# Modulation weights of a two-block network: one transfer and one tile for four k tiles instead of one

## The chip, the core and the metric

The kernel runs on one core of a Trainium2 chip, alone. The metric is device time in microseconds (us) of one execution of the whole program; lower is better. The engines of the core are named as the profile names them: PE is TensorE's matrix multiplication and PEld its weight load, DVE is VectorE, ACT is ScalarE, POOL is GpSimd, and SP is the engine from whose queue (SPq) nearly all DMA transfers of this kernel are issued, in order.

## The reference, cut to what matters

The whole network is a DiT-like stack of two blocks of two layers each (512 latent and 256 context tokens, model width 1024). Only the first layer of the first block, a gated delta net, is touched by the change. Ahead of every sublayer the reference modulates the normed tokens with shift, scale and gate vectors, which come from two conditioning vectors through a large matrix:

```
inputs['ada_w'] = nrm((DEPTH, D, 6 * D), D ** -0.5)     # [2, 1024, 6144], fp32: 48 MB
inputs['c'] = nrm((BATCH, D), 1.0)                      # conditioning of the latent tokens
inputs['c_ctx'] = nrm((D,), 1.0)                        # conditioning of the context tokens
...
shift, scale, gate, ... = split(silu(c) @ ada_w[l] + ada_b[l], 6)      # in words; for c and for c_ctx
```

So two vectors of 1024 numbers are multiplied with all of a 48 MB matrix. The product itself is tiny; what counts is that all 48 MB pass through SBUF and through the matrix engine once as moving data. The gated delta net around it projects the tokens to q, k, v and z (a 5-tap convolution and silu on q, k, v), and then runs a chunked recurrence over six chunks of 128 tokens in both directions, with a triangular inverse for each chunk.

## The kernel before, in words

**The modulation products.** The 12 sections of 1024 columns are made in 24 blocks of 512 columns (`ada_block`). A block needs the 1024 rows of the matrix, that is 8 k tiles of 128 rows. For each k tile, `raw_weights` (line 314 issues the transfer) loads a tile `araw` [128, 512] of 256 KB, and one fp32 product with a stationary operand of only 32 columns (`s4`, of which two columns are the two vectors) is made. k tile `kt` goes to column tile `kt % 4` of the array, 32 output partitions each, so that four products can run side by side if they stand next to each other in PE's queue and have their data. An fp32 product is two MATMUL instructions in the trace. All eight add up in one PSUM bank (`a`, in the first blocks also `g` or `i` by name), ACT copies the bank to `arow` (line 330), and four small products with `sel` add the four column tiles up. Every matmul of the kernel has line 163 (`mm`) and every transpose line 167.

**The buffers.** The first four blocks (shift and scale of the first layer, which everything waits for) take their tiles from the pool `stage`, 16 tiles of 256 KB. The other 20 blocks take theirs from `aw`, a ring of `ada_bufs` = 3 tiles. A tile is free again when its product is done, so from then on a new transfer waits on SPq for PE.

**Where the 20 blocks run.** They are `later` work: `deltanet` calls `fill(...)` between the projections, scans and inverses of the four pairs of heads, a block at a time (`ada_steps`). The order of the instructions on each engine is made by a scheduler ahead of the run, which moves the pieces among each other by priority (`scan_hp`, `inv_hp`) and by its own idea of when data is there. On the chip each engine then takes its list in order, and SPq issues its transfers in order too: what stands behind a waiting transfer waits with it.

**The other names.** `dn_project` makes q, k, v of two heads: PE products (g <- hh, wh and the like; high and low parts, 512 latent and 256 context tokens), then ACT and DVE convolve and apply silu. `sums` puts squares in a tile `acc` (one buffer), `dn_gate` puts silu(z) in `acc` too and stores it to DRAM (`zs`), and the convolved v stands in a tile `vT` (one buffer) until PE has transposed it (`dn_token_major`). `wr` are weights as loaded (ring of 2), `wh` and `wl` their high and low parts (made by ACT, line 203, and DVE, line 204; rings of 4). At the end `dn_output` fetches six heads' outputs from DRAM (`on`, two buffers, line 892; `z`, one buffer, line 894), multiplies them on DVE (line 895) and transposes them on PE; the last two heads go straight through `dn_direct`.

Of the kernel before, what the change touches and what calls it, by code (L numbers as in the profile page):

```python
# [21 lines left out]
P = 128  # L22
# [18 lines left out]
class Kernel:  # L41
    # how many steps of independent work go into the gaps of a chain, ring sizes, scheduling priorities
# [6 lines left out]
    ada_bufs = 3  # L49
# [18 lines left out]
    # ---------------------------------------------------------------- helpers  # L68
# [27 lines left out]
    def banks(self, **turns):  # L96
        """a tag takes the banks of these tags in turn (2: halves of s2)"""
        self.turns, self.rest = {k: itertools.cycle(v) for k, v in turns.items()}, None

    def psum(self, **nb):  # L100
        """(re)partition the 8 PSUM banks among tags"""
        if self.pb is not None:
            self.pb.release()
        self.nb = nb
        self.pb = self.pool("ps", 1, PSUM) if nb else None

    def setup(self):
# [17 lines left out]
        self.le = tri("le", -1, 1, ALU.is_ge)   # [p, f] = p <= f  # L125
        self.ge = tri("ge", 1, -1, ALU.is_ge)   # p >= f
        self.gt = tri("gt", 1, -1, ALU.is_gt)   # p > f
        self.lt = tri("lt", -1, 1, ALU.is_gt)   # p < f
# [5 lines left out]
    def open_w(self, raw, hi, unit, side):  # L134
        """rings of weight tiles: raw, high and low parts"""
        return unit, self.pool("wraw", raw, side=side), self.pool("whi", hi, side=side), self.pool("wlo", hi, side=side)
# [8 lines left out]
    def rsqrt(self, out, in_, mul, add, exponent=None):  # L145
        """out = (in_ * mul + add) ** -0.5 on GpSimd, tiny operands"""
# [11 lines left out]
    def exp_ln_tables(self):  # L158
        """the activation tables that hold both exp and ln, from here on"""
# [9 lines left out]
    def rows_to_cols(self, rows, tag, pool=None):  # L169
        """rows: DRAM APs [r, 128] -> const tile [128, sum r], whose columns self.finish_cols() fills"""  # L170
# [18 lines left out]
    def split(self, hi, lo, src, hi_eng):  # L189
        """hi + lo = src exactly, each with at most 12 significant bits"""  # L190
# [3 lines left out]
    def weights(self, src, a, mul=None):  # L194
        """DRAM view [128, a, unit // a] (times mul) -> hi, lo tiles of that shape"""
# [11 lines left out]
    # weights stationary: feature-major result, 256 output features at a time  # L207
# [3 lines left out]
    def gemm_steps(self, w, c0, groups, evac, ncol=256):  # L211
        """groups: lists of segments; a segment is (hi(kt), lo(kt), n). evac(j, [psum per segment])"""
# [12 lines left out]
    def ws_tile(self, ps, wk, j, segs, kts=range(NK)):  # L225
        """128 output features of the segments"""
# [6 lines left out]
    def gemm_halves(self, parts, segs):  # L233
        """the same of several (weights, first column, evac), where the last tokens come late: all products of the
        first segment go ahead"""
# [11 lines left out]
    # tokens stationary: token-major result, 512 output features at a time  # L247
# [14 lines left out]
    def ts_pair_steps(self, wk, hh, hl, t, out):  # L262
        """token tiles t, t + 1, 256 output features each, in the halves of a bank"""
# [16 lines left out]
    # ---------------------------------------------------------------- modulation  # L280
    def ada_setup(self):
# [11 lines left out]
        # column v of s4: vector v; the four column tiles of the array take a k tile each  # L293
# [3 lines left out]
        # sel[r, v]: rows that add up to vector v: v of each column tile, and the bias in row 2; then without the bias  # L297
# [10 lines left out]
    def raw_weights(self, src, a):  # L308
        if self.ada_own:
            raw = self.t(self.aw, [P, self.unit], "araw", bufs=self.ada_own)  # L310
        else:
            raw = self.t(self.stage, [P, self.unit], "araw", bufs=16)
        raw = raw.rearrange("p (a b) -> p a b", a=a)
        self.nc.sync.dma_start(out=raw, in_=src)
        return raw

    def ada_block(self, l, n, row):
        """products with columns n * 512 .. of ada_w[l] into row [128, 512], to be summed by sel"""
# [3 lines left out]
        per = self.unit // 512  # L322
        for u in range(NK // per):
            r0 = u * per * P
            raw = self.raw_weights(w[r0:r0 + per * P, n * 512:(n + 1) * 512].rearrange("(a p) m -> p a m", p=P), per)
            for a in range(per):
                kt = per * u + a
                r = slice(32 * (kt % 4), 32 * (kt % 4) + 32)
                self.mm(ps[r, :], self.s4[:, kt, :], raw[:, a, :], start=(kt < 4), stop=(kt >= 4))
        nc.scalar.copy(row, ps)  # L330

    def ada_cols(self, l, sec):
        """section sec of layer l, feature-major: [128, 8, 2] (lat, ctx)"""
# [13 lines left out]
    def ada_bc_store(self, l, sec, dst):  # L347
        """section sec of layer l to DRAM rows dst [2, 1024] (lat, ctx), to be read back on all partitions"""
# [12 lines left out]
    def load_bc(self, pool, row, tag, n=D):  # L361
        """a DRAM row [n] on all partitions"""
# [4 lines left out]
    # ---------------------------------------------------------------- gated delta net (layer 0)  # L367
# [3 lines left out]
    def load_transposed(self, x_src, ctx_src, xp):  # L371
        """the rows of x and ctx, feature-major: 8 tiles [128, 768]"""
# [21 lines left out]
    def deltanet(self, xp, xT, scratch, zs, gts, later):  # L394
        """normed, gated head outputs before norm_g go to scratch; returns the transposed y"""
# [7 lines left out]
        # shift, scale and the first products, in halves of the features  # L403
# [37 lines left out]
        # decay and beta  # L441
# [52 lines left out]
        def conv_silu2(blk, dst, ps):  # L494
            """dst = 2 silu(conv(x))"""
# [16 lines left out]
        for grp in range(4):  # L512
# [7 lines left out]
            # independent work for the gaps of the chains  # L520
# [26 lines left out]
    def dn_gate(self, half, w, hh, hl, onep, zs):  # L547
        """2 silu(z) of two heads, token-major, to DRAM"""
# [11 lines left out]
    def dn_project(self, grp, w, segs, one, onep, conv_silu2, beta, eg, fill, first):  # L560
# [8 lines left out]
        def sums(src, tag):  # L569
            """sums of squares per token, of twice the value"""  # L570
# [3 lines left out]
            # as rows, two chunks per column tile of the array; then transposed  # L574
# [32 lines left out]
        def ev_v(j, ps):  # L607
            vT = onep([P, W2], "vT", 1)
# [30 lines left out]
    def dn_tmp(self, one, shape):  # L639
        """one of a ring of 4 KB scratch tiles"""  # L640
# [8 lines left out]
    def dn_prepare(self, p, one, g):  # L649
        """inverses of both directions' triangular systems, and the q k products times the decays: their upper  # L650
        triangle is for direction 0, the lower one for direction 1"""
# [4 lines left out]
        for j, h in enumerate(heads):  # L656
            # decays between tokens j, i: a sum over an empty range in one of the two directions
# [34 lines left out]
    def dn_invert(self, Wt, one):  # L692
        """Wt[:, u] (unit triangular but for its diagonal; u < 12 upper, u >= 12 lower) -> its inverse, in place"""
# [7 lines left out]
        # [(b, i), u, j] -> [(b, u), i, j]: one matrix per partition  # L701
# [17 lines left out]
        # [0]: blocks of the inverse, [1]: their transposes; direction 0 was inverted transposed  # L719
# [8 lines left out]
        # 32 -> 64: source block row, target block row, per direction and pair  # L728
# [23 lines left out]
        # transposed 64-blocks: direction 0 in rows 0:64, direction 1 in rows 64:128  # L752
# [8 lines left out]
        # 64 -> 128  # L761
# [106 lines left out]
    def dn_store(self, p, O, one, scratch):  # L868
        """half the normed head outputs to DRAM"""
# [17 lines left out]
    # ---------------------------------------------------------------- shared pieces  # L887
    def dn_output(self, k, scratch, zs, yh, yl, yp, zp):
        """y = norm(o) * silu(z), transposed and split into yh, yl (norm_g applied on the way)"""
        nc = self.nc  # L890
        on = self.t(yp, [P, TOK], "on", bufs=2)
# [14 lines left out]
    def scaled_split(self, hi, lo, ps, scale):  # L906
        """hi + lo = ps * scale"""
# [39 lines left out]
    def proj_steps(self, w, xh, xl, k0, k1, tiles, evac, ncol=512):  # L947
        """token-major projection of k tiles k0 .. k1 of the transposed, split activations by w, in steps;
        evac(t, c0, psum[:, :ncol])"""
# [13 lines left out]
    def ln_stats(self, x, pool):  # L963
        """1 / std and mean per token"""
# [10 lines left out]
    def layernorm(self, x, pool):  # L975
        """x <- (x - mean) * rstd, per token"""
# [1287 lines left out]
```

## Time and profile before

| | |
|---|---|
| Time, median of three runs | 3865.22 us (3863.72 to 3866.85) |
| Profiled execution, first to last instruction (span) | 3858.7 us |
| PE busy over the span | 3740.8 us, 97% |
| DVE, ACT, POOL busy | 2343.5, 1541.7, 440.1 us |
| First 740 us of the span, where all modulation products run: PE busy | 701.67 us |
| ... of it with modulation products (araw) | 134.25 us |
| Transfers of araw | 192 of 256 KB |

The span is that of one profiled execution; the runs' median is 6.5 us above it. Times in the rows below are us from the span's start. PE "busy" is the time in which at least one matmul is under way; the matmuls are pipelined and overlap, so that what one costs the engine is read from the distance between its start and the start of what follows.

### The profile page before, as it was taken

What the parts mean: (1) busy time and instruction counts of PE and PEld (TensorE: products, weight loads), DVE (VectorE), ACT (ScalarE), POOL (GpSimd) and SP (SyncE); (2) the same over time, 40 slices, a digit from 0 to 9 for tenths busy, and PEclk for the clock granted to TensorE, in tenths of its full rate; (3) what the DMA queues carried; (4) which work ended last, traced back from release to release, by engine and by line L of the source; (5) the groups of instructions that cost most, each with busy time, mean ns of one, the idle gap of its engine ahead of it and who ended that gap; (6) DMA issues with size and microseconds to landing.
All of it is one profiled execution on the core that took longest, in us unless ns stands there. A gap on an engine that the chain in (4) does not pass through costs nothing.

```text
span 3858.7 us, 57682 instructions
## 1 busy us (share of the span) xinstructions
PE 3740.8 (97%) x23195; PEld 3033.0 (79%) x23195; DVE 2343.5 (61%) x3919; ACT 1541.7 (40%) x2836; POOL 440.1 (11%) x642
## 2 busy tenths in 40 slices
PE   8999999999999999998999999999999999999999
PEld 5675766888888877777888877788887888888887
DVE  3757655653333676677555656656666777556665
ACT  3444443332211244454222456544334655444332
POOL 3112211040000020003000102100000222100000
PEclk9999999999999999999999998999999999999999
DMA  4234234512122211113333213212332223223232
GB/s 166 77 96 132 88 118 126 175 61 66 56 65 66 69 59 33 34 50 91 98 97 91 86 55 106 65 60 88 99 96 86 72 67 106 87 66 93 91 95 82
DMA packets 248974, 329.47 MB, mean 85 GB/s; under 512 B 14408, under 2 KB 194988, under 8 KB 248705
## 3 DMA queue, kind: packets, MB, share of 16 engines
q1 hardware_dynamic: 248000, 325.40, 27.2%
q8 instruction: 182, 2.98, 0.3%
q14 instruction: 88, 0.71, 0.1%
q0 software_dynamic: 704, 0.37, 0.0%
HBM read 318.09 MB, written 7.63 MB: 84 GB/s over the span
## 4 chain that ended last, share of the span: by engine, by line
PE 83%; DVE 6%; ACT 4%; POOL 3%; issue 2%; DMA 1%; SPq 0%; ACTq 0%; POOLq 0%; DVEq 0%
PE g L163 41%; PE a L163 16%; PE o L163 13%; PE s L163 7%; PE i L163 2%; PE s L167 1%; PE a L167 1%; PE p L163 1%; DVE wl L204 1%; DMA araw<-in_ada_w_dram 1%; ACT wh L203 1%; ACT xr L1480 1%; ACT xr L1477 0%; DVE bst L968 0%; PE g L167 0%
## 5 line engine op out<-in xcount | busy, mean ns | idle before, releaser
L204 DVE TENSOR_TENSOR wl<-wr,wh 128x1024 fp32r<-128x1024 f32 (+1 forms) x508 | 587.6, 1164 | 435.8 <-ACT wh L203 420.8
L203 ACT CAST wh<-wr 128x1024 fp32r<-128x1024 f32 (+1 forms) x508 | 493.5, 981 | 783.6 <-PE o L163 373.1
L163 PE MATMUL g<-wh,fh 128*128 128x512 f32 x396 | 156.4, 395 | 0.0
L163 PE MATMUL g<-wh,fl 128*128 128x512 f32 x396 | 156.1, 395 | 0.0
L163 PE MATMUL g<-wl,fh 128*128 128x512 f32 x396 | 155.1, 392 | 0.0
L163 PE MATMUL g<-h2l,wh 128*128 128x512 f32 x352 | 138.0, 392 | 2.4 <-DVE h2l L1014 2.4
L163 PE MATMUL g<-h2h,wh 128*128 128x512 f32 x352 | 137.5, 392 | 0.0
L163 PE MATMUL g<-h2h,wl 128*128 128x512 f32 x352 | 137.1, 390 | 0.0
L163 PE MATMUL a<-araw,s 128*32 128x512 f32 x352 | 125.7, 617 | 6.2 <-DMA araw<-in_ada_w_dram 5.9
L163 PE MATMUL g<-hh,wh 128*128 128x512 f32 (+1 forms) x376 | 115.7, 363 | 1.7 <-ACT hh L421 1.5
L152 POOL TENSOR_SCALAR brs<-bmv 128x1 f32<-128x1 f32 x20 | 9.7, 484 | 932.1 <-DVE bmv L970 922.9
L163 PE MATMUL g<-hh,wl 128*128 128x512 f32 (+1 forms) x376 | 112.6, 358 | 3.5 <-DVE wl L204 3.5
L163 PE MATMUL g<-hl,wh 128*128 128x512 f32 (+1 forms) x376 | 114.0, 358 | 0.8 <-POOL hl L422 0.6
L1049 DVE TENSOR_TENSOR x<-g,x 128x512 f32<-128x512 f32 x120 | 82.5, 688 | 30.5 <-PE g L163 30.3
L163 PE MATMUL s<-k,q 128*128 128x384 f32 (+1 forms) x256 | 98.7, 440 | 0.0
L1186 DVE TENSOR_REDUCE nm<-s 128x1 f32<-128x768 f32 x64 | 61.1, 955 | 52.3 <-PE s L163 52.3
L163 PEld LDWEIGHTS g<-hh,wh 128*128 128x128 f32 x376 | 63.5, 193 | 35.5 <-issue 20.5
L163 PEld LDWEIGHTS g<-hl,wh 128*128 128x128 f32 x376 | 63.4, 192 | 32.6 <-issue 23.7
L163 PEld LDWEIGHTS g<-hh,wl 128*128 128x128 f32 x376 | 62.7, 192 | 32.4 <-issue 21.3
L163 PEld LDWEIGHTS g<-wh,fh 128*128 128x128 f32 x396 | 74.4, 188 | 17.4 <-ACT fh L2096 0.6
L1291 ACT CAST fh<-sg 128x768 fp32r<-128x768 f32 (+1 forms) x44 | 32.0, 726 | 138.9 <-DVE sg L1290 138.9
L163 PEld LDWEIGHTS g<-wl,fh 128*128 128x128 f32 x396 | 74.4, 188 | 16.6
(994 smaller groups left out, 11513.5 us busy)
## 6 DMA issues: line engine op xcount, KB each, us to landing
wr<-in_ffn_w_up_dram SPq DMA_DIRECT2D x132, 512.0 KB, 3.7
araw<-in_ada_w_dram SPq DMA_DIRECT2D x192, 256.0 KB, 3.1
wr<-in_ffn_w_down_dram SPq DMA_DIRECT2D x88, 512.0 KB, 3.7
wr<-in_ffn_w_gate_dram SPq DMA_DIRECT2D x44, 512.0 KB, 3.8
wr<-in_dn_w_in_dram SPq DMA_DIRECT2D x66, 256.0 KB, 2.8
wr<-in_xa_w_kv_dram SPq DMA_DIRECT2D x32, 512.0 KB, 3.9
wr<-in_hgrn_w_in_dram SPq DMA_DIRECT2D x32, 512.0 KB, 4.2
wr<-in_da_w_in_dram SPq DMA_DIRECT2D x24, 512.0 KB, 3.5
```

Of the source, the lines that this page charges most:

```text
L152: nc.gpsimd.tensor_scalar(out=out, in0=in_, scalar1=mul, scalar2=add, op0=MUL, op1=ADD)
L163: self.nc.tensor.matmul(out, lhsT=lhsT, rhs=rhs, start=start, stop=stop)
L167: self.nc.tensor.transpose(out, in_, self.ident[0:k, 0:k])
L203: nc.scalar.copy(hi, raw)
L204: nc.vector.tensor_tensor(out=lo, in0=raw, in1=hi.bitcast(F32), op=SUB)
L1049: nc.vector.tensor_tensor(out=a, in0=ps, in1=a, op=ADD)
L1186: nc.vector.tensor_reduce(out=nm, in_=s[cc][:, :, 0:384], axis=AX.XY, op=MAX, negate=True)
L1291: nc.scalar.copy(hi[j], sg[j])
L1480: nc.scalar.activation(y, x, AF.Copy, scale=rs)
```

## The change

A transfer now brings four k tiles at once: `araw` is [128, 4, 512], 1 MB, and a block takes two of them (`u` = 0 and 1). The four products of a tile go to the four column tiles of the array. There are 48 transfers instead of 192. The bytes, the products and what they add up to are the same. `stage` keeps its size (4 tiles of 1 MB for 16 of 256 KB). The ring in `aw` goes from three tiles of 256 KB to one of 1 MB. To make room for it, `vT` shares the one buffer of `acc`, and `on` has one buffer instead of two.

```
-    ada_bufs = 3
+    ada_bufs = 1
...
-    def raw_weights(self, src, a):
+    def raw_weights(self, src):
         if self.ada_own:
-            raw = self.t(self.aw, [P, self.unit], "araw", bufs=self.ada_own)
+            raw = self.t(self.aw, [P, 4, 512], "araw", bufs=self.ada_own)
         else:
-            raw = self.t(self.stage, [P, self.unit], "araw", bufs=16)
-        raw = raw.rearrange("p (a b) -> p a b", a=a)
+            raw = self.t(self.stage, [P, 4, 512], "araw", bufs=4)
         self.nc.sync.dma_start(out=raw, in_=src)
         return raw
...
-        per = self.unit // 512
-        for u in range(NK // per):
-            r0 = u * per * P
-            raw = self.raw_weights(w[r0:r0 + per * P, n * 512:(n + 1) * 512].rearrange("(a p) m -> p a m", p=P), per)
-            for a in range(per):
-                kt = per * u + a
-                r = slice(32 * (kt % 4), 32 * (kt % 4) + 32)
-                self.mm(ps[r, :], self.s4[:, kt, :], raw[:, a, :], start=(kt < 4), stop=(kt >= 4))
+        for u in range(2):
+            raw = self.raw_weights(w[512 * u:512 * u + 512, n * 512:(n + 1) * 512].rearrange("(a p) m -> p a m", p=P))
+            for a in range(4):
+                self.mm(ps[32 * a:32 * a + 32, :], self.s4[:, 4 * u + a, :], raw[:, a, :], start=(u == 0), stop=(u == 1))
...
-            vT = onep([P, W2], "vT", 1)
+            vT = onep([P, W2], "acc")
...
-        on = self.t(yp, [P, TOK], "on", bufs=2)
+        on = self.t(yp, [P, TOK], "on", bufs=1)
```

The scheduler makes a new order from this for the first fifth of the program. PE's list of 20359 instructions has 3431 that stand otherwise at its front; the last 16928 are the same in both, and the order on the other engines is the same behind the delta net too.

PE, fifth block of modulation products (the first from the ring in `aw`), among the products of a projection (g <- hh, wh are token products), before: some of the block's eight products stand alone or in twos.

```order
L163 MATMUL g_1736<-hh_56_263,wh_1713 128x512
L163 MATMUL g_1737<-hh_56_263,wh_1713 128x256
L163 MATMUL g_1736<-hl_64_271,wh_1713 128x512
L163 MATMUL a_1680<-araw_1693,s_12_112 32x512
L163 MATMUL a_1680<-araw_1696,s_12_112 32x512
L163 MATMUL g_1737<-hl_64_271,wh_1713 128x256
L163 MATMUL g_1736<-hh_56_263,wl_1714 128x512
L163 MATMUL g_1737<-hh_56_263,wl_1714 128x256
L163 MATMUL g_1736<-hh_57_264,wh_1719 128x512
L163 MATMUL a_1680<-araw_1699,s_12_112 32x512
L163 MATMUL g_1737<-hh_57_264,wh_1719 128x256
L163 MATMUL g_1736<-hl_65_272,wh_1719 128x512
```

PE, the same block after the change: the first four products stand together (x4), then come 29 token products (15 of 128x512 and 14 of 128x256, of which the last are shown), then the second four.

```order
L163 MATMUL g_1676<-hl_67_274,wh_1665 128x512
L163 MATMUL g_1677<-hl_67_274,wh_1665 128x256
L163 MATMUL g_1676<-hh_59_266,wl_1666 128x512
L163 MATMUL a_1632<-araw_1639,s_12_112 32x512 x4
L163 MATMUL g_1677<-hh_59_266,wl_1666 128x256
L163 MATMUL g_1676<-hh_60_267,wh_1665 128x512
```

What moved: products of k tiles that stood between token products now stand in fours. In 29 of the 44 fours behind the first two blocks nothing stands between the four; in 15 the first product stands apart from the other three. The first two blocks stand as eight in a row each.

SP, transfers at the same place, before: the ring's transfers of 256 KB, singly and in threes, among the weights `wr`.

```order
L200 DMA wr_1730<-in_dn_w_in_dram 128x2x256
L314 DMA araw_1693<-in_ada_w_dram 128x512
L314 DMA araw_1696<-in_ada_w_dram 128x512
L314 DMA araw_1699<-in_ada_w_dram 128x512
L200 DMA wr_1907<-in_dn_w_in_dram 128x2x256
L314 DMA araw_1702<-in_ada_w_dram 128x512
L314 DMA araw_1876<-in_ada_w_dram 128x512
L314 DMA araw_1879<-in_ada_w_dram 128x512
```

SP, the same place after the change: each `araw` has to wait until PE is through with the four products of the `araw` ahead of it.

```order
L200 DMA wr_1835<-in_dn_w_in_dram 128x2x256
L314 DMA araw_1639<-in_ada_w_dram 128x4x512
L200 DMA wr_1841<-in_dn_w_in_dram 128x2x256
L314 DMA araw_1816<-in_ada_w_dram 128x4x512
L349 DMA arow_1631<-in_ada_b_dram 1x512
L354 DMA gts_256<-arow_1649 2x512
L200 DMA wr_1847<-in_dn_w_in_dram 128x2x256
```

What moved: one transfer stands where up to four did, and weights, the bias row `arow` and the store `gts` stand right behind it.

SP at the end of the delta net, before: `on` and `z` of the six heads in turn, `on` one head ahead of `z`.

```order
L892 DMA on_7355<-osc_257 128x768
L894 DMA z_7357<-zs_258 128x768
L892 DMA on_7372<-osc_257 128x768
L200 DMA wr_7788<-in_dn_w_out_dram 128x2x256
L894 DMA z_7374<-zs_258 128x768
L892 DMA on_7389<-osc_257 128x768
```

SP at the same place after the change, the last four heads and the first of `dn_direct`: the `on` of a head stands behind its own `z` now.

```order
L890 DMA z_7120<-zs_258 128x768
L888 DMA on_7118<-osc_257 128x768
L890 DMA z_7137<-zs_258 128x768
L888 DMA on_7135<-osc_257 128x768
L890 DMA z_7154<-zs_258 128x768
L888 DMA on_7152<-osc_257 128x768
L876 DMA z_7175<-zs_258 128x768
```

What moved: a head's `on` is issued after the transposes of the head before it, no longer one head ahead.

## Rows read from the trace of the kernel before

**Rows 1.** The page, head and part 1: busy us (share of the span) and instructions.
```profile
span 3858.7 us, 57682 instructions
PE 3740.8 (97%) x23195; PEld 3033.0 (79%) x23195; DVE 2343.5 (61%) x3919; ACT 1541.7 (40%) x2836; POOL 440.1 (11%) x642
```

**Rows 2.** Windows, two stretches: length, PE PEld DVE ACT POOL busy, clock, DMA share, GB/s.
```profile
0.00:57.00 57.00, 45.06 (x196) 22.27 (x197) 13.49 (x32) 14.00 (x26) 19.87 (x45) 0.94 0.67 238
57.00:682.00 625.00, 604.83 (x4589) 429.06 (x4588) 400.27 (x947) 276.93 (x612) 113.70 (x130) 0.99 0.34 103
```

**Rows 3.** Windows of the same stretches, instructions on tile araw alone: PE, PEld busy.
```profile
0.00:57.00 57.00, 19.72 (x65) 2.99 (x66) 0.94 0.67 238
57.00:682.00 625.00, 114.53 (x320) 15.52 (x318) 0.99 0.34 103
```

**Rows 4.** Waits of PE from 57 to 682 us: total us, times, longest.
```profile
PE a L163 <- DMA araw<-in_ada_w_dram: 5.9, 6, 2.2
```

**Rows 5.** Timeline of PE: start us, us until the last one ends, instruction, [idle before].
```profile
15.50 1.04 PE L163 MATMUL a<-araw,s 128*32 128x512 f32 x2
...
22.73 2.22 PE L163 MATMUL i<-araw,s 128*32 128x512 f32 x16
...
147.05 0.51 PE L163 MATMUL g<-hh,wl 128*128 128x512 f32 x2
147.40 0.51 PE L163 MATMUL g<-hh,wh 128*128 128x512 f32 x2
...
151.20 1.06 PE L163 MATMUL a<-araw,s 128*32 128x512 f32 x6
152.19 0.50 PE L163 MATMUL g<-hh,wh 128*128 128x512 f32 x1
...
157.76 1.05 PE L163 MATMUL a<-araw,s 128*32 128x512 f32 x2
158.74 0.39 PE L163 MATMUL g<-hh,wh 128*128 128x256 f32 x1
...
678.72 1.04 PE L163 MATMUL a<-araw,s 128*32 128x512 f32 x2
```

**Rows 6.** Transfers: SPq's timeline; DMA share in 40 slices of 555.8 to 560.8 us; landing.
```profile
555.87 1.28 SPq L314 DMA_DIRECT2D araw<-in_ada_w_dram  x3
557.19 0.42 SPq L200 DMA_DIRECT2D wr<-in_dn_w_in_dram  x1
...
DMA  0000000059925597999989999999899999641000
DMA packets 704, 1.05 MB, mean 210 GB/s; under 512 B 64, under 2 KB 320, under 8 KB 704
...
DMA to landing us min/median/max: 2.6/3.0/4.8
```

**Rows 7.** Timeline of PE, then a window: length, PE busy, granted clock, DMA share, GB/s.
```profile
453.94 0.62 PE L163 MATMUL g<-hh,wl 128*128 128x512 f32 x2 [2.06 <-DVE wl L204]
...
455.00:458.40 3.40, 3.40 (x13) 0.50 0.82 220
```

**Rows 8.** Tile vT: count, durations in ns min/median/max, first and last start.
```profile
L503 DVE SCALAR_TENSOR_TENSOR vT<-xin,convw,vT x32: 1002/1022/2233, 115.9 to 611.0; 128x772 f32<-128x772 f32 x32
L501 ACT ACTIVATE vT<-xin,convw x8: 932/938/942, 114.9 to 606.5; 128x772 f32<-128x772 f32 x8
L504 ACT ACTIVATE vT<-vT x8: 846/847/850, 121.1 to 615.0; 128x772 f32<-128x772 f32 x8
```

**Rows 9.** The last two of six heads: timelines of DVE and PE; tile on's landing.
```profile
719.27 0.95 DVE L895 TENSOR_TENSOR on<-on,z 128x768 f32<-128x768 f32 x1
...
723.41 0.95 DVE L895 TENSOR_TENSOR on<-on,z 128x768 f32<-128x768 f32 x1
...
720.37 0.85 PE L167 MATMUL g<-ident,on 128*128 128x128 f32 x6 [0.37 <-DVE ms L863]
...
DMA to landing us min/median/max: 3.6/3.6/3.6
```

## The prediction

> **What bounds the kernel now.** I read the page first: PE is busy for 97% of the span, every other engine for far less [rows 1]. Such an average need not hold in the stage that changes, so the windows come next. The modulation products run in the first 682 us. From 57 to 682 us PE is busy for 604.83 of 625 us, DVE for 400.27, ACT for 276.93, and the DMA engines have a share of 0.34 [rows 2]. PE thus idles for 20.2 us in 625 although the scan and the inverse of the delta net are long chains: the scheduler has enough independent products to lay between their links. In this stage a us taken off PE is a us off the end, as long as that cover lasts. The same windows for the tile araw alone say what the modulation costs PE: 19.72 us before 57 us and 114.53 us after it, 134.25 in all [rows 3]. Little of this is waiting: 5.9 us for transfers of araw, 6 times [rows 4].
>
> The timeline shows why it is so much. One k tile alone (two MATMULs) starts at 157.76 and the next product at 158.74: 0.98 us. Three k tiles side by side (six MATMULs) start at 151.20 and the next product at 152.19: 0.99 us [rows 5]. Three cost what one costs, because they work in different column tiles of the array. Sixteen MATMULs, eight k tiles, last 2.22 us at 22.73 us, in two rounds over four column tiles [rows 5], so the fourth column tile works beside the others as well. I counted such runs in the timeline from the one at 15.50 to the one at 678.72 [rows 5]: 123 of them; 81 are of one k tile, 24 of two, 16 of three, and the first two blocks have one of seven and one of eight. Behind these there are 120 runs for 22 blocks and a piece, 5.5 a block, where two would do.
>
> **What the change takes away.** In the new order the first two blocks stand as eight and eight again. Of the other 44 fours, 29 stand together and 15 are torn in one and three; that makes 59 runs instead of 120. 61 runs at 0.98 us are 59.8 us of PE. The byte count is the same, so the DMA engines have as much to move. SPq has 144 issues less, which is worth nothing: it isn't waited for by itself.
>
> The Trainium skill (TensorE: Matmul & The Clock Gate, Measured speedup vs the span model) gives 2.38 times for three column tiles; the rows here show 3 x 0.98 / 0.99 = 2.97 times. By the page's figure a run of three would take 3 x 0.98 / 2.38, an estimate of 1.24 us, and 59 runs of no less would cost 15 us more than at 0.98, a gain of 45 us instead of 60. The measurement decides here, since these are the same products with the same operands.
>
> **What it adds: one buffer.** The next 1 MB can be asked for only when the last of four products has read the tile, and PE takes its list in order: if the second four come to their turn too early, PE stands, with all token products behind them. So the question is how much PE work the order puts between two fours, against how long a refill takes. Work: 15 products of 128x512 and 14 of 128x256 between the two fours shown in the order; a pair of one each takes 0.35 us (147.05 to 147.40, [rows 5]), so 14 pairs and one more 128x512 of about 0.23 make 5.1 us. Summing the rows of the order in this way for all 39 refills of the ring gives about 5.5 us or less for 16 (most near 5.1), 5.7 to 6.5 for 6, and more for the other 17, up to over 40. Refill: no transfer of 1 MB of araw is in the trace, but one MB issued in four pieces from 555.87 on is: its packets are through by the 37th slice of 0.125 us, at 560.4, 4.6 us after the first issue [rows 6]. One issue should do no worse. 4.6 us plus a few tenths for semaphores against 5.1: it just fits, where nothing stands in front. Bounds: below, 3.0 us, as one 256 KB transfer lands in the median (then nothing waits). Above: the slices show the MB moving for 3.6 us (from 556.8), 0.9 for each 256 KB; the median landing with 0.75 MB more is 5.7, and with 256 KB of weights in front 6.6 us [rows 6]. That would be 1.5 us at 16 places and 0.6 at 6, 28 us. A wait of 2 us is followed by 3.4 us at a granted clock of 0.50, the 1.2 GHz level (453.94 and 455.00, [rows 7]), 1.7 us lost each time; two or three of these make it 32 us. I take 0.5 us at 16 places: 8 us, nearer to the piece that was one MB than to the sum of pieces. Behind a waiting araw on SPq stand weights `wr`; they have rings of their own, and araw waited in the same queue before.
>
> **vT in acc.** Each of 8 v tiles lives for 0.94 (ACT) + 4 x 1.02 (DVE) + 0.85 us (ACT) plus its transposes, 7 us [rows 8], and the silu of the gate or a square waits for it, or it for them. 0 us if PE has other products (it has, see above), 28 us if PE stood for one life in each of four pairs of heads. DVE and ACT are in order, so a little will show: 3 us.
>
> **on with one buffer.** The last two heads follow each other on DVE at 4.14 us (719.27, 723.41). With one buffer the cycle is landing 3.6, multiplication 0.95, transposes 0.85, with some 0.2 for issue and semaphores: 5.6 us [rows 9]. The heads before lie under the scan's last steps, so 1.5 us for two heads: 3 us, on the path, for the output projection waits for the last heads. If the scan ended earlier, four heads: 6 us; if all lay under it, 0.
>
> **Thinner cover.** With 60 us less to lay between the links of the chains, PE waits more often. Its 20.2 us of idle time could shrink by the 5.9 for araw or double. I take 6 us.
>
> **Sum.** 60 - 8 - 3 - 3 - 6 = 40 us off. Against the profiled span of 3858.7 that is 3818.7; the runs' median stands 6.5 us above the span, so **3825 us**. Everything behind the delta net has the same order and the same times.
>
> **The rivals.**
>
> *The chains take over.* DVE's 400.27 us in a stage that shrinks to some 570 is 70% instead of 64%, and scan and inverse can't be shortened. For it: PE's waits at 2.06 for `wl` [rows 7] show that DVE is late here and there already. Against it: 70% is still far from full. If idle time doubles (20 us) and vT costs 8: 60 - 8 - 8 - 3 - 20 = 21 off, 3844.
>
> *The refill is too long: slower.* Place: the second four of each block. The gain before waits is 60 - 12 = 48 us; spread over the 22 tight refills that is 2.2 us each, so it decides at a refill of about 7.3 us. The slowest landing of 256 KB, 4.8, with 0.75 MB more is 7.5 us [rows 6]; if every tight refill were like that (SPq held by a store that waits for ACT does the same), 22 waits of 2.4 us and 16 halved clocks of 1.7 us make 80 us: 32 more than the gain, 3897. Against it stand the 4.6 us. The Trainium skill's rule speaks for it: Trainium Kernel Development and Optimization, Best Practices, asks for double buffers to overlap transfer and compute, which this change gives up. By that rule alone all 39 refills of 4.6 us would lie open, 179 us; the order with its 5.1 us of other products shows why I don't take it so.
>
> *Column tiles run side by side less well in fours* (the page's 2.38 times): 15 us less gain, 3840; rows of three at 0.99 us stand against it.
>
> *No effect:* the time of this stage isn't PE's but that of the scheduler's chains, and PE only fills it. Then the waits go up by what the runs go down, 3865. Against it: PE's 20 us of idle time.
>
> **Chances.** Forecast 0.73; chains take over 0.11; fours less well 0.02; no effect 0.06; refill too long 0.08. What a measurement of this kernel can tell from no change is about 0.2%, 8 us. So faster 0.86, same 0.06, slower 0.08. The range: the lower end is 60 off and the 5.9 us of waits gone with no costs, 3799; the upper end takes the refill's upper bound (32), 6 for `on`, 3 and 6 for the rest: 13 off, 3852. It leaves out the last two cases (0.14) and little of the rest.
>
> **What would show it.** In the changed profile: windows of araw alone near 75 us instead of 134; runs of eight MATMULs followed by the next product after 1.0 us; PE's stage ends some 40 us earlier; PE's waits for araw of some 8 us in total, at second fours; `on` at 5.6 us from head to head at the end. It is wrong if PE's waits for araw exceed 20 us (refill over 6 us), if PE's waits for DVE and ACT grow by what araw gives back, or if a run of four costs clearly more than 1.0 us.

## The result and the profile after

The changed kernel takes **3804.43 us** (median of 4 runs, 3801.96 to 3806.98) against 3866.03 us of the kernel before, run beside it; ratio 0.9844, 95% interval 0.9832 to 0.9856. A second time, in a later comparison, it was 3804.63 against 3863.16 us, ratio 0.9843 (0.983 to 0.9856). The gain is 61.6 and 58.5 us; 40 us were forecast. Single runs that a much lower clock had lengthened (one each of three kernels below) are left out of all ratios and ranges; they stay in the medians, which would be lower by at most 1.2 us without them.

The page of the changed kernel, head and part 1, answers to [rows 1]:

```profile
span 3805.3 us, 57443 instructions
PE 3681.0 (97%) x23195; PEld 3032.8 (80%) x23195; DVE 2338.4 (61%) x3919; ACT 1540.7 (40%) x2834; POOL 436.5 (11%) x642
```

PE is still what is full, with 59.8 us less of work in a span that is 53.4 us shorter. The windows of as much work, counted in MATMULs (4791 now, 4785 before), which ends at 622.5 us instead of 682, answer to [rows 2]; one four of k tiles stands behind them. Columns are length, PE, PEld, DVE, ACT and POOL busy, granted clock, DMA share, GB/s:

```profile
0.00:50.00 50.00, 35.64 (x188) 22.19 (x188) 13.18 (x30) 14.08 (x26) 18.38 (x44) 0.86 0.79 282
50.00:622.50 572.50, 547.58 (x4603) 423.08 (x4603) 397.11 (x955) 276.23 (x613) 113.21 (x130) 0.99 0.35 111
```

and those of the tile araw alone to [rows 3]; columns are length, PE, PEld busy, granted clock, DMA share, GB/s:

```profile
0.00:50.00 50.00, 10.05 (x64) 1.45 (x64) 0.86 0.79 282
50.00:622.50 572.50, 57.11 (x312) 8.23 (x312) 0.99 0.35 111
622.50:690.00 67.50, 2.10 (x8) 0.29 (x8) 0.92 0.55 184
```

The modulation products cost PE 69.3 us where they cost 134.25; about 75 were forecast. PE's idle time in the stage is 572.50 - 547.58 = 24.9 us, where it was 20.2 [rows 2]. Its waits from 50 to 622.5 us (total, times, longest) answer to [rows 4]; with the last four, at 625 us, those for araw are 8.3 us, 8 times:

```profile
PE a L163 <- DMA araw<-in_ada_w_dram: 7.5, 7, 2.2
PE g L163 <- DVE wl L204: 3.2, 4, 0.9
PE i L163 <- ACT invR L734: 2.1, 3, 0.8
PE p L163 <- ACT acc L569: 2.0, 2, 1.6
```

PE's timeline around two fours of k tiles (eight MATMULs each; start, us until the last one ends), to be read beside [rows 5]:

```profile
179.88 0.51 PE L163 MATMUL g<-hl,wh 128*128 128x512 f32 x2
180.23 0.40 PE L163 MATMUL g<-hh,wh 128*128 128x512 f32 x1
180.56 1.06 PE L163 MATMUL a<-araw,s 128*32 128x512 f32 x8
181.55 0.50 PE L163 MATMUL g<-hl,wh 128*128 128x512 f32 x1
181.89 0.75 PE L163 MATMUL g<-hh,wl 128*128 128x512 f32 x3
...
301.42 1.94 PE L163 MATMUL a<-araw,s 128*32 128x512 f32 x8 [1.92 <-DMA araw<-in_ada_w_dram]
```

A four costs 0.99 us from its start to the next one's, as one k tile does. The rows show one thing more: the 128x512 token product ahead of the run is 0.33 us from its start to the run's (180.23 to 180.56), the one behind it 0.34 us from the next (181.55 to 181.89). Over the whole stage the median distance from a 128x512 token product to the next start is 0.23 us among its like (470 of them), 0.33 ahead of a run (9) and 0.34 behind one (8); for 128x256 it is 0.12 (923), 0.21 (9) and 0.22 (20). Before, the medians are the same within 0.01 us. So a run costs its 0.98 us and 0.2 us more at its two edges, **1.17 us** (0.976 and 0.198 before rounding). The row at 301.42 is one of the waits for a refill, and the run behind it is at half the clock, the 1.2 GHz level (1.94 us).

Counted as for [rows 5], there are 61 runs where there were 123: two of eight, 29 of four, 15 of three, 15 of one. From the first MATMUL to the point from where PE's two lists are the same, the kernel before takes 693.3 us and the changed one 633.5, 59.8 less. Behind that point 6.4 us are given back (the spans are only 53.4 us apart), some 4 of them where `on` is fetched (below).

### The profile page after: what moved, and what is told of

Its sections match the earlier page's. It is cut to its first block, busy times and chain, and to the rows that moved or that the text cites. A ratio compares the mean times of both kernels' runs of the same rounds, so it can differ in the third digit from the quotient of the medians.

```text
span 3805.3 us, 57443 instructions
## 1 busy us (share of the span) xinstructions
PE 3681.0 (97%) x23195; PEld 3032.8 (80%) x23195; DVE 2338.4 (61%) x3919; ACT 1540.7 (40%) x2834; POOL 436.5 (11%) x642
## 4 chain that ended last, share of the span: by engine, by line
PE 82%; DVE 7%; ACT 4%; POOL 3%; DMA 2%; issue 2%; SPq 0%; ACTq 0%; POOLq 0%; DVEq 0%
PE g L163 41%; PE a L163 14%; PE o L163 13%; PE s L163 7%; PE i L163 2%; DMA araw<-in_ada_w_dram 1%; PE s L167 1%; PE a L167 1%; PE p L163 1%; DVE wl L204 1%; ACT wh L203 1%; ACT xr L1476 1%; ACT Wt L721 0%; DVE bst L964 0%; ACT xr L1473 0%
## 5 line engine op out<-in xcount | busy, mean ns | idle before, releaser
L163 PEld LDWEIGHTS g<-wh,fl 128*128 128x128 f32 x396 | 74.4, 188 | 16.4 <-DVE fl L2093 0.4
L1286 DVE TENSOR_TENSOR sg<-g,sg 128x512 f32<-128x512 f32 x33 | 22.8, 691 | 98.0 <-PE g L163 98.0
```

Of the source, the lines that this page charges most:

```text
L163: self.nc.tensor.matmul(out, lhsT=lhsT, rhs=rhs, start=start, stop=stop)
L1286: nc.vector.tensor_tensor(out=s, in0=p[:, 0:n], in1=s, op=MUL)
```

## The experiments

Two theories were set against each other. **R**: what counts is how many runs of araw products stand in PE's list, for products side by side share one run's time. **T**: the gain is that of long transfers (1 MB, 48 issues for 192). A *round* below is a run, or each pass of a longer one over the same column tiles; what the runs take beyond 0.98 us per round is waiting (or a lower clock) inside them: 3.2 us in the kernel before, 5.4 us in the changed one.

**All products in one column tile.** From the changed kernel, with the same 1 MB transfers; the copy of the bank and the sums at the end read 32 rows instead of 128 (not shown).

```
-                self.mm(ps[32 * a:32 * a + 32, :], self.s4[:, 4 * u + a, :], raw[:, a, :], start=(u == 0), stop=(u == 1))
+                self.mm(ps[0:32, :], self.s4[:, 4 * u + a, :], raw[:, a, :], start=(u + a == 0), stop=(u == 1 and a == 3))
```

Expected: 

> The changed kernel, but all products of a block go to the first column tile of the array and add up there (32 output partitions instead of 128, bias and sums read from these). Same transfers, same tiles, same sums. Theory R (the gain is the number of runs of products, each 0.98 us because column tiles work side by side): 192 products no longer share a run; in this kernel's order they stand in 105 runs, and with some 0.86 us for each product more in a run PE needs about 178 us for them instead of 69: some 109 us slower than the changed kernel, about 3913 us, slower than the kernel before. Theory T (the gain comes from 48 large transfers instead of 192, less waiting on SPq and DMA): 3800 to 3815 us, as the changed kernel.

Measured: 3926.49 us (3924.38 to 3932.45), ratio 1.0169 (1.0155 to 1.0183): 122 us over the changed kernel, with the same transfers. A pair in one column tile, in PE's timeline:

```profile
149.86 1.90 PE L163 MATMUL a<-araw,s 128*32 128x512 f32 x4
151.70 1.13 PE L163 MATMUL i<-qk 128*128 128x256 f32 x4
```

1.84 us for two products where the fours above take 0.99. T falls. R (3913 us) was 13 us short. By its own count, 105 first products at 0.98 us and 87 further ones at 0.86 are 178 us, 111 more than the 67 of the changed kernel's runs; the 44 runs more (105 for 61, the scheduler tore them) are 9 us at the edges: 120.

**The room alone.** The kernel before with `vT` in `acc` and one buffer of `on`; transfers, tiles and ring as before.

```
-            vT = onep([P, W2], "vT", 1)
+            vT = onep([P, W2], "acc")
...
-        on = self.t(yp, [P, TOK], "on", bufs=2)
+        on = self.t(yp, [P, TOK], "on", bufs=1)
```

Expected: 

> The kernel before with the two edits that make room alone: vT in the buffer of acc, and one buffer for on. Runs of araw products stay 123. The prediction's terms: 3 us for vT and 3 us for on, 3866 + 6 = 3872 us. From the changed trace, where the gain falls by 3.8 us between the start of the delta net's tail and its end and nothing is seen of vT: 3870 us. If the edits cost nothing: 3866 us.

Measured: 3868.96 us (11 runs), ratio 1.0015 (1.0006 to 1.0024), 4 us over before by the medians and 6 by the ratio (2 to 9 by the interval). To the point from where the lists are the same it takes 694.0 us instead of 693.3, so `vT` costs 0.7; the rest, 3 to 5 us, lies behind it, where `on` is.

**Four transfers to a tile.** From the changed kernel; the tile of four k tiles is filled by four issues of 256 KB.

```
-        self.nc.sync.dma_start(out=raw, in_=src)
+        for k in range(4):
+            self.nc.sync.dma_start(out=raw[:, k, :], in_=src[:, k, :])
```

Expected: 

> The changed kernel with each tile of four k tiles filled by four transfers of 256 KB instead of one of 1 MB; tile, ring and products as in the change. The order has 116 runs of araw products instead of 61, since a product can go as soon as its own quarter has landed. Theory R: 55 runs more at 0.98 us, 54 us slower than the changed kernel, about 3858 us, most of the gain gone. Theory T': one tile with one buffer is what counts, not the transfer: 3804 us. If transfers as such were the gain, this would lose it too, so this run tells the tile from the transfer, and the next ones tell runs from transfers.

Measured: 3871.38 us, ratio 1.0019 (1.0009 to 1.0028). The whole gain is gone (13 us slower than R said), and so are the fours: 116 runs. With pieces that come one by one, the scheduler's list has each product about where its piece is due. Taken from the room kernel's 3869, 7 runs less give 8 us, 6 us more of waiting inside the runs (9.6 for 3.6) and 3 us behind the point from where the lists are the same take them back.

**Products joined.** From the changed kernel, products 2 to 4 of each four at a higher priority, so that none is torn: 46 runs.

```
+                with self.hp(3500 if a else 0):
                     self.mm(ps[32 * a:32 * a + 32, :], ...
```

Expected: 

> The changed kernel with the second to fourth product of a tile given a higher priority, so that nothing comes between the four: 46 runs instead of 61, transfers the same. Theory R: 15 runs less at 0.98 us, 14.7 us faster than the changed kernel, about 3790 us. Theory T: no change, 3804 us. A rival: the fours then wait longer for their transfers, since the token products that stood in between are no longer there; PE's waits for araw, 8.3 us in the changed kernel, would grow by about as much, 3800 to 3806 us.

Measured: 3799.02 us (3796.47 to 3803.49), ratio 0.9836 (0.9823 to 0.985): 5 us under the changed kernel by the medians and 3 by the ratios, whose intervals overlap; not 15. PE's timeline has the rest, at second fours:

```profile
293.25 1.94 PE L163 MATMUL a<-araw,s 128*32 128x512 f32 x8 [3.98 <-DVE invt L709]
295.11 1.01 PE L163 MATMUL g<-hh,wh 128*128 128x512 f32 x2
...
430.07 1.93 PE L163 MATMUL a<-araw,s 128*32 128x512 f32 x8 [4.12 <-DMA araw<-in_ada_w_dram]
431.93 1.01 PE L163 MATMUL g<-hh,wl 128*128 128x512 f32 x2
```

The longest wait in the changed kernel is 2.2 us, here two are about 4, each followed by work at half the clock (a pair of token products in 1.01 us for 0.51). PE is idle some 8 us more up to where the lists are the same, and busy 10 to 11 us less, where 15 runs at 1.17 are 17.6. The clock has a part in this. PE's windows from 50 to 635 us, first of the changed kernel, then here (length, busy, granted clock, DMA share, GB/s):

```profile
50.00:635.00 585.00, 558.36 (x4668) 0.99 0.35 112
50.00:635.00 585.00, 551.33 (x4684) 0.97 0.36 112
```

The 0.02 of 585 us are some 10 us of PE's work. Where the long waits come from, PE's last products ahead of the refill and SPq's timeline show, again first the changed kernel, then here:

```profile
291.21 1.06 PE L163 MATMUL a<-araw,s 128*32 128x512 f32 x8
...
291.06 4.80 SPq L870 DMA_DIRECT2D osc<-O  x2
295.95 0.39 SPq L314 DMA_DIRECT2D araw<-in_ada_w_dram  x1
```

```profile
280.92 1.06 PE L163 MATMUL a<-araw,s 128*32 128x512 f32 x8
...
281.37 6.19 SPq L871 DMA_DIRECT2D osc<-O  x2
287.66 0.38 SPq L314 DMA_DIRECT2D araw<-in_ada_w_dram  x1
```

The products that read the tile last had ended at 292.3 and 282.0 us, but the refill stands on SPq behind two stores of the scan's outputs (`osc` <- `O`) and is asked for 3.7 and 5.7 us later; from there to its products it is 5.5 and 5.6 us (301.42 and 293.25, where the profile names DVE's `invt` for the wait). The other long wait of each kernel (2.2 us at 434.79, 4.1 at 430.07) follows a refill asked for 5.4 and 5.3 us late, behind stores `zs` and weights. By these rows it is the stores ahead of a refill that make it late, in both kernels. That what lay between the parts of a torn four is then missing as cover, and makes the same waits longer here, is argued and was not tried.

**Four small buffers.** The room kernel with `ada_bufs = 4`, 256 KB each: 110 runs.

Expected: 

> The kernel before with the two room edits (vT in the buffers of acc, one buffer of on) and the 12 KB that they free spent on a fourth 256 KB buffer of araw; the transfers and the tiles stay those of before. PE's list has 110 runs of araw products where the kernel before has 123. Theory R (a run of products side by side costs 0.98 us, and only the number of runs counts): the kernel with the room edits alone took 3869 us, less 13 x 0.98 = 12.7 us, 3856 us (0.9975 of before). Theory T (what pays is one long transfer of 1 MB, and more buffers of 256 KB give none of it): 3869 us. Rival W (products of a run still wait for the last of several transfers, as in the kernel with four transfers to a tile, which got nothing from 7 runs fewer): 3864 to 3869 us.

Measured: 3866.8 us (10 runs), ratio 1.0007 (0.9997 to 1.0017). R (0.9975) is out; Rival W fits, and T (3869 us, 1.0015) lies inside the interval too, so this run does not part those two. By the ratios 3 of the thirteen runs' 15 us are left. The runs hold 4 us more waiting (7.7 for 3.6), and PE's waits for `acc` and `vd` grow by 4 us (3.1 and 1.6 us, where the room kernel has 0.4 and 0.2). Up to the point from where the lists are the same the trace is 5.4 us ahead of the room kernel's; 2.7 of them are lost again while `on` is fetched.

**Twos.** The changed kernel with tiles of two k tiles, 512 KB, in a ring of two: 85 runs.

```
-    ada_bufs = 1
+    ada_bufs = 2
...
-            raw = self.t(self.aw, [P, 4, 512], "araw", bufs=self.ada_own)
+            raw = self.t(self.aw, [P, 2, 512], "araw", bufs=self.ada_own)
...
+        for u in range(4):
...
+            for a in range(2):
+                kt = 2 * u + a
+                r = slice(32 * (kt % 4), 32 * (kt % 4) + 32)
```

Expected: 

> The kernel after with tiles of two k tiles, 512 KB each, in a ring of two: the same SBUF, twice the transfers, 85 runs of araw products where the kernel after has 61 and the one before 123. Theory R: 3869 - 38 x 0.98 = 3832 us (from after: 3804 + 24 x 0.98 = 3828 us), PE's araw products take about 92 us up to where the lists become the same. Theory T (the length of the transfer counts): half the pieces, half the gain at most, 3835 to 3850 us. Rival W (two buffers instead of one take away the waits for refills): PE waits 4 us or less for araw where after waits 8.3 us, and 3824 us.

Measured: 3831.66 us (3830.04 to 3832.32), ratio 0.9913 (0.9898 to 0.9928). R said 3832 and 92 us for the products; the windows of araw (to 50 and to 647 us, columns as above) add up to 93.2:

```profile
0.00:50.00 50.00, 13.83 (x64) 2.19 (x64) 0.93 0.78 277
50.00:647.00 597.00, 79.38 (x320) 11.11 (x320) 0.99 0.35 108
```

The waits for araw are 7.3 us, 10 times: two buffers of half the size save PE almost nothing of them. 24 runs at 1.17 are 28 us, against 27 measured between the medians.

**Four transfers, products joined.** Both edits together: 96 runs, no transfer over 256 KB.

Expected: 

> The kernel with four 256 KB transfers to each tile of four k tiles, and products 2 to 4 of each four at a higher priority, so that they stand closer in PE's list: 96 runs where the kernel with four transfers alone has 116 and took 3871 us. No transfer of araw is longer than 256 KB. Theory R (only the number of runs counts): 3871 - 20 x 0.98 = 3852 us, PE's araw products 20 us less. Theory T (one transfer of 1 MB is what pays): 3866 to 3871 us. Rival W (products that are pulled together wait on PE for the later pieces): 3858 to 3866 us, with PE's waits for araw up from 7.6 us to 12 us or more.

Measured: 3860.38 us (10 runs), ratio 0.999 (0.9981 to 0.9999): 11 us under the kernel with four transfers alone, where 20 runs should give 23. PE's timeline shows where the others are:

```profile
211.34 1.05 PE L163 MATMUL a<-araw,s 128*32 128x512 f32 x2 [0.29 <-DMA araw<-in_ada_w_dram]
213.35 1.05 PE L163 MATMUL a<-araw,s 128*32 128x512 f32 x2 [0.96 <-DMA araw<-in_ada_w_dram]
```

These two stand next to each other in PE's list and use different column tiles, but the second piece lands later, so each has 0.98 us of its own, with 0.96 us of idle time between them. Runs hold 24.3 us of waiting, for 9.6: 15 us of the 23. The named wait for araw misses most of it (7.1 us for 7.6). So it is not the neighbours in the list but being ready together that pays, and one transfer for four products gives both.

**The kernel before once more.** For its profiled span.

Expected: 

> The kernel before once more, for a second profile of it. Its first profile has a span of 3858.7 us where its timed runs' median is 3866 us; if that execution was a fast one by chance, this profile's span is 3864 to 3868 us and PE's clock steps lie elsewhere; if profiled executions of this kernel are shorter than timed ones, it is 3857 to 3860 us again.

Measured: span 3860.1 us, own time 3861.81; its timed runs beside it 3860.02 to 3869.98, median 3863.57. Two profiled executions lie below the medians, by 3.5 us here and 6.5 the first time. 1.7 us of either is no chance: every run on record takes 1.7 to 2.2 us longer than its own span (here 3861.81 for 3860.1). With two of them it stays open whether the other 1.8 and 4.8 us are.

**The changed kernel once more, with two buffers of `on`, and with both edits.** SBUF holds no second `on` beside the 1 MB tile; in that stage the tile itself is free.

```
-        on = self.t(yp, [P, TOK], "on", bufs=1)
+        on = self.t(yp, [P, TOK], "on", bufs=1) if k % 2 == 0 else \
+            self.t(self.aw, [P, 4, 512], "araw", bufs=1).rearrange("p a n -> p (a n)")[:, 0:TOK]
```

Expected, the changed kernel: 

> The kernel after once more, beside the next two on the same chip: 3804 us (0.984 of before). Its profiled span, 3805.3 us the first time, falls anywhere from 3798 to 3806 us, as the timed runs do (3802 to 3807 us).

Expected, two buffers of `on`: 

> The kernel after, with the second buffer of on given back: every second on lies in the one buffer of araw, which is free in that stage, so that PE's list and the products are those of after. Theory R (one buffer of on costs 4 us, by the stage from where the lists are the same, 44.3 us before against 48.2 us after): 3800 us, 0.1% under after, and PE's wait for on at line 891 falls from 4.6 us to 2 us or less. Rival (that wait hides behind the other work of the gaps, and the 4 us are the clock's): 3804 us.

Expected, both edits: 

> The kernel after with both of its costs eased: products 2 to 4 of each four at a higher priority (46 runs of araw products instead of 61) and two buffers of on. Theory R: the kernel with the priority alone took 3799 us, less 4 us for on, 3795 us, 0.25% under after. Rival (each was noise, or the waits for the chains' results that came up in the kernel with the priority take it back): 3799 to 3804 us.

Measured on one chip: 3804.63 (span 3803.9), 3801.74 (3796.24 to 3808.27) and **3793.72** us (ratio 0.9813, 0.9801 to 0.9826), the best of all kernels here, 11 us under the changed kernel; R said 3795. The middle one's interval (0.9823 to 0.9851) does not part it from the changed kernel; DVE's timeline of the last heads does. First the changed kernel (first profile), then the one with two buffers, and last the kernel before:

```profile
632.52 0.96 DVE L891 TENSOR_TENSOR on<-on,z 128x768 f32<-128x768 f32 x1 [1.66 <-ACT O L840]
...
660.54 0.96 DVE L891 TENSOR_TENSOR on<-on,z 128x768 f32<-128x768 f32 x1 [0.21 <-DMA on<-osc]
667.22 0.96 DVE L891 TENSOR_TENSOR on<-on,z 128x768 f32<-128x768 f32 x1 [3.04 <-DMA on<-osc]
...
676.87 1.66 DVE L879 SCALAR_TENSOR_TENSOR O<-O,ms,z 128x128 f32<-128x128 f32 x6 [0.49 <-DMA z<-zs]
```

```profile
632.14 0.96 DVE L892 TENSOR_TENSOR on<-on,z 128x768 f32<-128x768 f32 x1 [1.81 <-ACT vd L819]
...
658.65 0.95 DVE L892 TENSOR_TENSOR on<-on,z 128x768 f32<-128x768 f32 x1
662.91 0.96 DVE L892 TENSOR_TENSOR araw<-araw,z 128x768 f32<-128x768 f32 x1
...
672.05 1.66 DVE L879 SCALAR_TENSOR_TENSOR O<-O,ms,z 128x128 f32<-128x128 f32 x6 [1.53 <-DMA z<-zs]
```

```profile
692.09 0.96 DVE L895 TENSOR_TENSOR on<-on,z 128x768 f32<-128x768 f32 x1 [1.67 <-DMA z<-zs]
...
732.90 1.67 DVE L883 SCALAR_TENSOR_TENSOR O<-O,ms,z 128x128 f32<-128x128 f32 x6 [0.66 <-DMA z<-zs]
```

With one buffer the last of the six heads takes 6.68 us and DVE stands 3.04 for `on`; with two it takes 4.26. The eight heads take 44.35, 39.91 and 40.81 us from first to last: by the traces one buffer of `on` costs 4.4 us against two in the changed kernel, and 3.5 against the kernel before; the runs alone are too few to show it. PE's wait for what `on` brings (line 167) falls from 4.6 us (2.8 in the second profile) to 0.8, as R said. In the kernel with both edits the price of a refill is seen whole. SPq's timeline at one of the waits, and then PE's:

```profile
284.19 6.18 SPq L871 DMA_DIRECT2D osc<-O  x2
290.47 0.38 SPq L314 DMA_DIRECT2D araw<-in_ada_w_dram  x1
```

```profile
296.50 1.94 PE L163 MATMUL a<-araw,s 128*32 128x512 f32 x8 [4.42 <-DVE gi L711]
```

The profile names DVE's `gi`, but DVE had been handing on links of the inverse all the while and araw was asked for only at 290.47, behind two stores; that is 6.0 us ahead of the products, about what a 1 MB transfer takes. That the wait is the refill's is read from these rows, not from a run that took it away.

## Why the prediction was right, point by point

The mechanism, the sign and the order of the terms were as forecast, and the time lies in the range, 5 us above its lower end, which took no costs at all; the gain was half as large again as the sum's 40 us. Nothing cancelled: what was taken away came out larger, what was added smaller in all (11 us for 20), and the base added some 8 us.

- **What the change takes away: 59.8 us.** The new order's runs were counted rightly (61); 62 fell away and not 61, for behind the first two runs there are 121 before (123 less two), not 120. The runs' own time fell from 125.7 to 67.2 us. The term was too small: it priced a run by the distance from its start to the next start, and left out the 0.2 us by which its two neighbours stretch, 12 us for 62 runs. By that it would be 70 us; PE's busy time up to where the lists are the same fell by 66.4 us (663.9 to 597.5).
- **The refill: 8 us.** PE's waits for araw rose from 5.9 to 7.5 us in the stage, 8.3 with the last four, a few of them followed by half the clock; 16 places at 0.5 us were too many. A 1 MB transfer lands after 5.2 us in the median (the page's list of issues), not the 4.6 of the four pieces [rows 6], yet the cover mostly held: at nine refills the products start only 5.1 to 5.4 us after the tile's last reader has ended, and the waits named there are 0.2 us or less. The two longest waits (1.9 and 2.2 us) follow the two refills that were asked for latest, 3.7 and 5.4 us after the last reader, behind stores on SPq. The sum had no term for that; the rival *refill too long* names it in brackets.
- **vT: 3 us.** 0.7 by the room kernel. A wait of 2.0 us for `acc` is new; PE has other products elsewhere.
- **`on`: 3 us.** 3.5 to 4.4 us by the traces. The step that was off is the cycle of 5.6 us, where the last head took 6.68: it took the landing of before, 3.6 us [rows 9]; in the changed kernel `on` is issued at 662.65 and DVE takes it at 667.22, 4.6 us, behind that head's own `z` in SPq.
- **Thinner cover: 6 us.** All idle time up to where the lists are the same rose by 6.7 us (29.4 to 36.0), refill and vT included; 17 were forecast for the three.
- **The base.** 66.4 - 6.7 - 4.4 are 55.3 us, and the spans differ by 53.4; some 2 us more are lost behind the delta net, where the lists are the same. The other 8 us of the 61.6 are in no row: the median of before lay 7.3 us over its profiled span in this comparison, that of the changed kernel 0.9 us under its own, so the 6.5 us that were carried over from the one to the other did not hold. The second pair of profiles is 56.2 us apart, its medians 58.5.

*Refill too long*: it did not come, though the mechanism exists; the joined kernels pay more of it, at waits of 3.5 to 4.4 us, three of them read above as refills held behind stores. *Chains take over*: idle time rose by 4.7 us in the stage, not 20; PE's waits for DVE's `wl` even fell (5.2 to 3.2 us). *Fours less well*: 0.976, 0.989 and 0.996 us are the medians for runs of one, three and four, 2.96 times for three column tiles and 3.9 for four; the 2.38 times for three in the Trainium skill (TensorE: Matmul & The Clock Gate, Measured speedup vs the span model) do not hold for these products. *No effect*: PE's busy time and the end moved together, 59.8 and 53.4 us.

## What to carry to other kernels

Small products in different column tiles cost one product's time only if they are ready together; where an order is made ahead by due times, bring their operands in one transfer, or the order tears them apart, and a higher priority alone makes them wait on the engine. Price a torn run by its own distance and by what its neighbours lose beside it (0.98 and 0.2 us here). A single large buffer is bearable where each refill (5.2 us here) is covered by other work of the same queue, and where no store that waits stands ahead of it in the DMA queue (the two longest waits here); before pulling products closer, count what that takes from the cover.

## What was not expected of the hardware

- A token product next to a 32-column fp32 run takes 0.09 to 0.11 us longer on either side, whatever its width (0.12 to 0.21 and 0.22 us; 0.23 to 0.33 and 0.34 us). Why was not tried.
- In one column tile the first product of a run costs 0.98 us, each further one 0.86 us (0.976, 1.834, 2.692, 3.551 us for runs of one to four): nearly no gain from standing together.
- One transfer of 1 MB lands in 5.2 us in the median, 512 KB in 4.4 and 256 KB in 3.1 (of those whose landing the traces tell: 6, 28 and 26): four times the bytes in 1.7 times the time.
